# Split SiLU-multiply: the first tile's store as one DMA over 128 partitions instead of five strided pieces

## The chip, the cores and the metric

The kernel runs on one core of a Trainium2 chip. The metric is device time in microseconds (us) of one execution. Three runs of the kernel before gave 470.19, 470.32 and 470.40 us; the median is 470.32 us.

The core has engines that work side by side, each with its own instruction stream: ScalarE (ACT in the profile) for activation functions, VectorE (DVE) for elementwise work, SyncE (SP), which here only starts transfers, and two that do nothing that matters here. Sixteen DMA engines move data between the device memory (HBM) and the on-chip memory of 128 partitions (SBUF). A transfer is started by an instruction on SP or ACT; SP's transfers stand in the queue that the profile calls q1, ACT's in q10, and both queues are worked off by the same sixteen engines.

## The reference

The input `x` has the shape 32 x 512 x 2048 in float32. With `x1` the first 1024 columns and `x2` the last 1024:

```python
silu_x1 = x1 * (1 / (1 + np.exp(-x1)))
return (silu_x1 * x2).astype(np.float32)
```

So 134.2 MB are read, each element once, and 67.1 MB are written.

## The kernel before

The 32 x 512 rows are taken as 16384 rows of 2048 numbers and cut into 16 tiles of 1024 rows. A tile lies on 128 partitions with K = 8 rows on each, so partition p of a tile holds eight neighbouring rows of the input: 64 KB in one piece on the way in, and 32 KB on the way out, since the output rows are half as long. A load is thus 8 MB, a store 4 MB. There are two input buffers `xt` and two output buffers `ot` (lines 58 and 59).

The order of the work is written out by hand in the loop (lines 101 to 120), and each engine executes its own instructions in that order:

- `load(i)` (line 82) is issued by SP. `load(0)` and `load(1)` come ahead of the loop; `load(0)` is even moved ahead of the program's first barrier (line 10). In tile i, after the store, `load(i + 2)` is issued; it goes into the buffer that tile i has just been read from, so it waits for tile i's last multiplication.
- `silu` (line 86) runs on ACT, from `xt` into `ot`. It waits for the load of its tile and, from tile 2 on, for the store of tile i - 2, which has to have left the `ot` buffer.
- `mul` (line 93) runs on DVE, in place on `ot`, with the second half of `xt`.
- the store (line 112) is issued by ACT, after the tile's last multiplication. ACT works in order, so the next tile's `silu` comes behind this issue.

Tile 0 is computed in four chunks of two rows (`KC_EDGE = 2`), tiles 1 to 14 in one piece, and tile 15 in two halves (`KS = 4`) with a store for each half (line 120).

The store of tile 0 alone is split. The list `OPENING` (line 49) has five pairs of a partition slice and a row slice. In order, the pieces are: rows 0 and 1 of every fourth partition from 0 (32 partitions, 256 KB); rows 0 to 3 of every fourth partition from 2 (512 KB); rows 4 to 7 of the same partitions (512 KB); rows 2 to 7 of every fourth partition from 0 (768 KB); and all rows of the odd partitions (64 partitions, 2048 KB). The first piece needs only the first chunk of tile 0 and the second only the first two chunks, so these can be issued before the tile is complete. With the five pieces the program has 37 DMAs: 16 loads, 5 pieces, 14 whole stores and 2 half stores.

Of the kernel before, what the change touches and what calls it, by code (L numbers as in the profile page):

```python
# [1 line left out]

# [4 lines left out]


def issue_ahead_of_the_first_barrier(nc):

    head, body = nc.main_func.blocks[:2]
    load = next(ins for ins in body.instructions if type(ins).__name__ == "InstDMACopy")
    at = next(
        j for j, ins in enumerate(head.instructions)
        if ins.engine == load.engine and type(ins).__name__ == "InstDrain"
    )
    body.instructions = [ins for ins in body.instructions if ins.name != load.name]  # L20
    head.instructions = head.instructions[:at] + [load] + head.instructions[at:]


@with_exitstack
def kernel(
    ctx: ExitStack,
    tc: tile.TileContext,
    x: bass.AP,
    out: bass.AP,
):  # L30

    nc = tc.nc
    P = nc.NUM_PARTITIONS

    x_flat = x.flatten_outer_dims()  # L40
    out_flat = out.flatten_outer_dims()
    num_rows, in_cols = x_flat.shape
    half = in_cols // 2
    dt = x_flat.dtype

    K = 8
    KC_EDGE = 2
    KS = 4
    OPENING = [
        (slice(0, None, 4), slice(0, 2)),  # L50
        (slice(2, None, 4), slice(0, 4)),
        (slice(2, None, 4), slice(4, None)),
        (slice(0, None, 4), slice(2, None)),
        (slice(1, None, 2), slice(None)),
    ]
    PLAN = [K] * (num_rows // (P * K))

    in_pool = ctx.enter_context(tc.tile_pool(name="in_pool", bufs=2))
    out_pool = ctx.enter_context(tc.tile_pool(name="out_pool", bufs=2))

    plan = []
    row = 0
    for k in PLAN:
        plan.append((row, k))
        row += P * k
    assert row == num_rows
    n_tiles = len(plan)

    def view(flat, i):
        row0, k = plan[i]  # L70
        return flat[row0:row0 + P * k].rearrange("(p k) d -> p k d", k=k)

    nc.at_finalize(issue_ahead_of_the_first_barrier)


    ctx.enter_context(tc.manual_schedule())

    loaded = {}

    def load(i):  # L80
        xt = in_pool.tile([P, K, in_cols], dt, name="xt")
        nc.sync.dma_start(out=xt[:, :plan[i][1], :], in_=view(x_flat, i))
        loaded[i] = xt

    def silu(ot, xt, c, ce):
        nc.scalar.activation(  # L86
            out=ot[:, c:ce, :],
            in_=xt[:, c:ce, :half],
            func=mybir.ActivationFunctionType.Silu,
        )  # L90

    def mul(ot, xt, c, ce):
        nc.vector.tensor_mul(  # L93
            out=ot[:, c:ce, :],
            in0=ot[:, c:ce, :],
            in1=xt[:, c:ce, half:],
        )

    load(0)
    load(1)  # L100
    for i in range(n_tiles):
        xt = loaded.pop(i)
        ov = view(out_flat, i)
        ot = out_pool.tile([P, K, half], dt, name="ot")
        if i < n_tiles - 1:
            kc = KC_EDGE if i == 0 else K
            for c in range(0, K, kc):
                silu(ot, xt, c, c + kc)
                mul(ot, xt, c, c + kc)

            for ps, ks in OPENING if i == 0 else [(slice(None), slice(None))]:
                nc.scalar.dma_start(out=ov[ps, ks], in_=ot[ps, ks])
            if i + 2 < n_tiles:
                load(i + 2)
            continue
        for c in range(0, K, KS):
            silu(ot, xt, c, c + KS)
            mul(ot, xt, c, c + KS)
        for c in range(0, K, KS):
            nc.scalar.dma_start(out=ov[:, c:c + KS], in_=ot[:, c:c + KS])  # L120


# [1 line left out]
_INS = ['x']  # L124
_OUTS = [((32, 512, 1024), 'float32')]


# [23 lines left out]
```

## Time and profile before

| what | value |
|---|---|
| median of three runs (lowest, highest) | 470.32 us (470.19, 470.40) |
| span of the profiled execution, first to last instruction | 468.39 us |
| that span below the median of the runs | 1.93 us |
| time of all packets, as a share of 16 DMA engines over the span | q1 66.4%, q10 33.2% |
| mean rate | 430 GB/s |
| DVE busy, ACT busy | 139.3 us, 114.1 us |
| idle time of ACT that a store's landing ended | 305.8 us, 14 times |
| from issue to landing, median | load 35.1 us, whole store 42.2 us |
| `silu` of a whole tile, `mul` of a whole tile | 7.03 us, 8.69 us |

For the profiled execution the span is given and no device time of its own; what lies around the span is taken as the 1.93 us between it and the median of the runs. All times inside an execution count from the span's start.

A few terms. A packet is what one DMA engine moves at a stretch: in a load, one partition's 64 KB; in a whole store, one partition's 32 KB. With 128 partitions over 16 engines each engine has 8 packets of every load and of every whole store. Behind them each engine has one more record of 4 bytes, which reports that the engine's part is done; it is called the closing entry here. So a load or a whole store is 9 entries on each engine, and its landing is the report of the last of the 16. In the view of the DMA queues, "packets" counts the entries of all sixteen engines that start in the chosen window.

### The profile page before, as it was taken

How to read it: one execution, taken by the hardware profiler on the slowest of the kernel's cores; microseconds unless marked ns; L12 is line 12 of the kernel's file. 1: busy time of each engine (PE TensorE's matmuls, PEld its weight loads, DVE VectorE, ACT ScalarE, POOL GpSimd, SP SyncE). 2: the span in 40 equal slices, each digit the busy share in tenths (PEclk: the TensorE clock that was granted, in tenths of full speed). 3: DMA queues.
4: the chain of work that ended last, by engine and by line, in shares of the span. 5: the costliest groups of instructions: out<-in, count | busy, mean ns of one | idle time of the engine just before them, and what ended most of it. 6: DMA issues, size and time to landing. Idle time of an engine off the chain costs nothing.

```text
span 468.4 us, 185 instructions
## 1 busy us (share of the span) xinstructions
DVE 139.3 (30%) x20; ACT 114.1 (24%) x21; POOL 0.2 (0%) x4
## 2 busy tenths in 40 slices
DVE  0070600704207042070520605116061150602543
ACT  1142305005050050601406014060230602306060
POOL 0000000000000000000000000000000000000000
DMA  9899999999999999999999999899999899999998
GB/s 442 364 470 425 448 403 403 493 403 403 448 465 431 403 442 409 493 403 414 437 448 448 403 448 465 386 448 439 411 493 442 372 439 493 403 448 403 428 423 358
DMA packets 4880, 201.33 MB, mean 430 GB/s; under 512 B 592, under 2 KB 592, under 8 KB 592
## 3 DMA queue, kind: packets, MB, share of 16 engines
q1 hardware_dynamic: 2304, 134.22, 66.4%
q10 hardware_dynamic: 2576, 67.11, 33.2%
HBM read 134.22 MB, written 67.11 MB: 430 GB/s over the span
## 4 chain that ended last, share of the span: by engine, by line
DMA 72%; DVE 14%; ACT 11%; DVEq 1%; issue 0%
DMA out_dram<-ot 63%; DVE ot L93 14%; ACT ot L86 11%; DMA xt<-in_x_dram 9%; DVEq L146 1%
## 5 line engine op out<-in xcount | busy, mean ns | idle before, releaser
L93 DVE TENSOR_TENSOR ot<-ot,xt 128x8192 f32<-128x8192 f32 (+2 forms) x20 | 139.3, 6983 | 321.1 <-ACT ot L86 321.1
L86 ACT ACTIVATE ot<-xt 128x8192 f32<-128x8192 f32 (+2 forms) x20 | 112.8, 5661 | 340.2 <-DMA out_dram<-ot 305.8
L86 ACT ACT_TABLE_LOAD x1 | 1.3, 1283 | 0.8 <-PEq L135 0.8
L135 POOL MEMSET const-bfloat16-1.0<- 128x1 bf16 x1 | 0.1, 102 | 0.0
L135 POOL MEMSET const-uint8-127<- 128x1 uint8 x1 | 0.1, 102 | 0.0
L135 POOL MEMSET const-float32-1.0<- 128x1 f32 x1 | 0.1, 99 | 0.0
L135 POOL MEMSET const-float32-0.0<- 128x1 f32 x1 | 0.1, 98 | 0.2 <-issue 0.2
## 6 DMA issues: line engine op xcount, KB each, us to landing
out_dram<-ot ACTq DMA_DIRECT2D x14, 4096.0 KB, 42.2
out_dram<-ot ACTq DMA_DIRECT2D x3, 2048.0 KB, 6.9
out_dram<-ot ACTq DMA_DIRECT2D x2, 512.0 KB, 17.6
out_dram<-ot ACTq DMA_DIRECT2D x1, 768.0 KB, 28.2
xt<-in_x_dram SPq DMA_DIRECT2D x16, 35.1
out_dram<-ot ACTq DMA_DIRECT2D x1, 256.0 KB, 11.3
```

Of the source, the lines that this page charges most:

```text
L86: nc.scalar.activation(out=ot[:, c:ce, :], in_=xt[:, c:ce, :half], func=mybir.ActivationFunctionType.Silu,)
L93: nc.vector.tensor_mul(out=ot[:, c:ce, :], in0=ot[:, c:ce, :], in1=xt[:, c:ce, half:],)
L135: nc = _bacc.Bacc("TRN2", target_bir_lowering=False, num_devices=1)
L146: with _tile.TileContext(nc) as tc:
```

## The change

The list `OPENING` goes, and tile 0 is stored like tiles 1 to 14: one DMA over all 128 partitions, issued after the tile's last multiplication. The four chunks in which tile 0 is computed stay. The program has 33 DMAs.

```diff
-    OPENING = [
-        (slice(0, None, 4), slice(0, 2)),
-        (slice(2, None, 4), slice(0, 4)),
-        (slice(2, None, 4), slice(4, None)),
-        (slice(0, None, 4), slice(2, None)),
-        (slice(1, None, 2), slice(None)),
-    ]
     PLAN = [K] * (num_rows // (P * K))
...
-            for ps, ks in OPENING if i == 0 else [(slice(None), slice(None))]:
-                nc.scalar.dma_start(out=ov[ps, ks], in_=ot[ps, ks])
+            nc.scalar.dma_start(out=ov, in_=ot)
             if i + 2 < n_tiles:
                 load(i + 2)
             continue
```

## The prediction

> **What bounds the kernel now.** I read the page first: the DMA row and the queue rows.
>
> ```profile
> span 468.4 us, 185 instructions
> ...
> DMA  9899999999999999999999999899999899999998
> ...
> q1 hardware_dynamic: 2304, 134.22, 66.4%
> q10 hardware_dynamic: 2576, 67.11, 33.2%
> ```
>
> The 16 DMA engines are busy 99.6% of the span. The bytes do not change, so the kernel can become slower only where these engines run dry, and faster only by what they lose besides moving bytes. The place where they could run dry is the end, so I read the timeline there: after the last load nothing but stores is left, and the two half stores of tile 15 must be computed while older stores keep the engines busy.
>
> ```profile
> 439.57 0.34 ACTq L112 DMA_DIRECT2D out_dram<-ot  x1
> 448.01 7.12 ACT L86 ACTIVATE ot<-xt 128x4096 f32<-128x4096 f32 x2 [17.20 <-DMA out_dram<-ot]
> 451.66 8.76 DVE L93 TENSOR_TENSOR ot<-ot,xt 128x4096 f32<-128x4096 f32 x2 [12.13 <-ACT ot L86]
> 456.12 4.67 ACTq L120 DMA_DIRECT2D out_dram<-ot  x2
> ```
>
> The last tile's silu starts at 448.01, its first half store is issued 8.11 us later, and the packet records have its first packet 0.85 us after that, at 456.97. Tile 14's store ends at 456.85 on the first of the engines and at 457.29 on the last. The gap is at most 0.12 us: the cover just suffices. So the question is how many store packets are left when the last load is in.
>
> Next I read the queues with windows, to see how they share an engine. From 20.9 to 31 us:
>
> ```profile
> q1 hardware_dynamic: 80, 4.19, 99.0%
> ...
> out_dram<-ot ACTq DMA_DIRECT2D x1, 512.0 KB, 15.7
> out_dram<-ot ACTq DMA_DIRECT2D x1, 256.0 KB, 11.3
> ```
>
> 80 load entries, 5 on each engine (load 0's closing entry and four packets of load 1), and no row for q10, though two pieces were issued in this window. From 31 to 443.5 us:
>
> ```profile
> q1 hardware_dynamic: 2080, 121.64, 68.1%
> q10 hardware_dynamic: 2080, 57.15, 32.1%
> ```
>
> 2080 entries each, 130 on each engine: the queues take strict turns, one entry each, closing entries included. From 444.7 to 445.3 us:
>
> ```profile
> q10 hardware_dynamic: 16, 0.52, 202.3%
> q1 hardware_dynamic: 16, 0.00, 1.5%
> ```
>
> Here the last load closes, with 0.00 MB: its 16 closing entries (the packet records: at 444.75 on the first engine, 445.19 on the last; landing 445.54).
>
> **A count that fixes the end.** Each engine has 16 x 9 = 144 load entries. n of them have gone by when the first store packet gets its turn; from there each load entry goes with one store entry. So when load 15 closes, 144 - n store entries are done. Before, n = 8 (load 0) + 5 = 13, so 131. Up to and including tile 14 there are 17 entries of the five pieces (12 packets of 8 to 32 KB, 5 closing entries: 272 of the page's 2576 over 16) and 14 x 9 = 126, in all 143. Left: 12 entries, of which 10 are packets of 32 KB and two close. The records show just these: from the closing of load 15 to tile 14's end is 457.29 - 445.19 = 12.10 us, 10 packets of 1.21.
>
> After the change, tiles 0 to 14 have 15 x 9 = 135 store entries. Left when load 15 closes: 135 - (144 - n) = n - 9, one of them closing: **r = n - 10 packets**, instead of 10. The four missing closing entries and the four missing small packets bring the store queue eight turns forward; a later start gives some back.
>
> **What n becomes.** The first piece was issued at 26.02 and moved first at 31.02 to 31.42 (16 engines). The new store is issued at 32.62, when the last multiplication of tile 0 ends; that is when the third piece is issued now, and nothing ahead of it changes (DVE runs its four chunks back to back). Until it joins, loads go on alone at 2.418 us a packet: packet ends at 30.72, 33.14, 35.56, 37.98, 40.39 (0.39 later on the last engine) mean n = 13, 14, 15, 16, 17. How long a whole store needs to join a running load queue is not in the trace. The nearest row is the first piece: it missed the turn 2.29 to 2.67 us after its issue and took the one at 5.00 to 5.40. The lower bound from elsewhere is the 0.85 us of the first half store, on engines that had nothing else to do. For the new store the turn at 35.56 to 35.95 is 2.94 to 3.33 us after issue, that at 37.98 to 38.37 is 5.36 to 5.75. By the first piece the delay lies between 2.67 and 5.00, so the second turn is safe and the first is reached only by a delay under 3.33, which is (3.33 - 2.67) / 2.33 = 28% of that stretch. I take the second: **n = 16, r = 6**. Ends kept: n = 15 and n = 17.
>
> **The sum.**
> 1. Load 15 closes later by the (10 - 6) store packets that now come before it: 4 x 1.213 = 4.85 us. It lands at 445.54 + 4.85 = 450.39.
> 2. Today the last silu waits for tile 13's store (447.99) and not for the load. With r = 6 that store is out earlier, so the load decides: the silu starts at 450.41 instead of 448.01, and the first half store's first packet comes at 456.97 + 2.40 = 459.37.
> 3. All bytes up to tile 14 are still moved by 456.85 to 457.29, so the engines idle for about 2.1 us (last engine) to 2.4 us (first). The half stores then run as now. The last engine sets the end, but also starts level with the others: before, starts 0.33 us apart became ends 0.21 apart (466.81 to 467.02). From 459.37, 9.72 to 9.84 us of packets give 469.09 to 469.21 against 467.02: **+2.1 to +2.2, taken as +2.15 us**, at most 2.40.
> 4. Off it goes what the pieces cost the DMA engines. Three rounds of load packets around the pieces take 2.704, 2.606 and 2.709 us instead of 2.418 (those that start at 28.30, 31.32 and 36.64), 0.77 us in all; whole stores later show nothing of the kind. The new store is also the first to join, so one excess of 0.29 may stay: I take -0.48, bounds 0 and -0.77.
> 5. ACT saves four issues: the five take 0.55 + 0.48 + 0.48 + 0.62 + 0.63 us, one whole store 0.36. It then waits 14.73 us for load 1, which hides this: 0. Closing entries take 0.009 us each: 0. Load 2's issue on SP waits for the same multiplication, at 32.62: 0. Compute in the middle: a tile's store is issued 15.79 us after its silu starts, and r + 1 = 7 entries of the older store, in turns of 3.63 us with loads, cover 25.4 us: 0; with r = 5 still 21.8.
>
> Sum: 468.39 + 2.15 - 0.48 = 470.06 for the span, and with the 1.93 us around it **472.0 us** (470.32 + 1.67 = 471.99). Bounds of this case: 470.32 + 2.15 - 0.77 = 471.7 and 470.32 + 2.40 = 472.7.
>
> The Trainium skill, "DMA: Bandwidth & Descriptors", section "Rules for kernel authors", advises one 128-partition transfer where transfers to disjoint partitions share the engines, so by it the change is right or neutral; that weighs each DMA, not the order in which two queues drain. The same page, "Queues, rings and completion order", has an engine drain a packet of some 9 to 17 descriptors from one queue before it switches; the rows above differ, one entry each. If a whole DMA of 9 entries went per turn, tile 14's whole store would be left at the end, the loss would vanish, and the time would be about 470.
>
> **The rivals.**
> - *The store joins a turn earlier on at least one engine* (n = 15, r = 5). The landing of each load waits for its slowest engine, so one engine is enough. One more packet, 1.21 us: 471.99 + 1.21 = 473.2 (bounds 472.9 to 473.9). For it: the turns of the 16 engines are spread over 0.39 us, and 2.94 is near 2.67. Against: most of the possible delays.
> - *Earlier still* (n = 14): +1.21 again, 474.4. It needs a delay under 0.9 us, which only the idle engines of the tail show.
> - *A turn later* (n = 17, r = 7): 1.21 less, 470.8. The delay must exceed 5.36 us; the first piece allows at most 5.40 on its last engine, and a store of 128 rows may be slower to start.
> - *The other side: the tail stays covered.* The place is the wait before the last silu. With r = 8 or more the load no longer decides: (10 - 8) x 1.213 = 2.43 us, just the 2.45 between load 15's and store 13's landings. Then only step 4 remains: 470.32 - 0.48 = 469.8 (469.6 to 470.3). It decides from n = 18 on: the store would have to miss the turn at 40.4 too, some 7.8 us after its issue, or the middle would have to reset the order of the queues. Against: no wait there leaves an engine idle now, so nothing resets it. That the pieces do nothing for the end gives the same numbers.
>
> **How the numbers follow.** Chances: r = 6, 0.50; r = 5, 0.30; r = 4, 0.05; r = 7, 0.07; tail covered or no effect, 0.08. A measurement of this kernel tells about 0.2% (0.94 us) from no change. The first three are slower by more than that: 0.85. r = 7 (+0.5) lies within it, as does most of the last case: 0.13 same. Faster by over 0.94 us would need more than all of the 0.77: 0.02. The likeliest gives 472.0. The range: r = 6 and r = 5 hold 0.80 and reach from 471.7 to 473.9; since the low side has more cases I go down to 471.0, into r = 7, and up to 474.0.
>
> **What would show it.** In the changed kernel: q10's first packets at 37.98 to 38.4 (35.6 would be the first rival, 40.4 the third); load 15's landing near 450 (449.9 with step 4) and the last silu released by the load, no longer by a store; the chain through the loads; some 2 us without any packet near 457 to 459; one long load packet before the first store packet instead of three. Wrong would be: the last silu still released by a store, the queues not in strict turns, or a dry stretch in the middle.

## The result and the profile after

The changed kernel takes 473.38 us (median of 14 runs, 473.01 to 474.15); beside it the kernel before took 470.33 us (14 runs). The ratio is 1.0057, with a 95% interval of 1.0041 to 1.0073: 3.05 us slower by the medians, where 1.67 were forecast. The direction and the range held (471.0 to 474.0); the likeliest case was 1.4 us too low. In the experiments below, two of the twelve runs of two by rows (486.0 and 486.5 us) were disturbed and are left out of its ratio and range, and beside the last three kernels some runs of the kernel before were long (up to 477.19 us), which pulls their ratios below what the medians give. The profiled execution of the changed kernel took 473.47 us with a span of 471.14 us.

The page after, its DMA row and its queues:

```profile
span 471.1 us, 177 instructions
...
DMA  9999999999999999999999899999999999999978
...
q1 hardware_dynamic: 2304, 134.22, 66.1%
q10 hardware_dynamic: 2448, 67.11, 33.0%
```

The store queue has 128 entries fewer (8 on each engine, as counted), the bytes are the same, and the slice that lost is the last but one, 7 where there was a 9. The timeline after, from tile 14's last multiplication:

```profile
437.90 0.34 ACTq L104 DMA_DIRECT2D out_dram<-ot  x1
451.04 7.12 ACT L79 ACTIVATE ot<-xt 128x4096 f32<-128x4096 f32 x2 [21.89 <-DMA xt<-in_x_dram]
454.69 8.76 DVE L86 TENSOR_TENSOR ot<-ot,xt 128x4096 f32<-128x4096 f32 x2 [16.82 <-ACT ot L79]
459.15 4.67 ACTq L112 DMA_DIRECT2D out_dram<-ot  x2
```

Tile 14's store is even issued 1.67 us earlier than before (437.90 against 439.57), but the last silu starts 3.03 us later, and what releases it is now the load and no longer a store. In the list of waits this has turned round for the whole kernel; the line that named the stores with 305.8 us is gone, and this one stands in its place (total, times, longest):

```profile
ACT ot L79 <- DMA xt<-in_x_dram: 343.3, 16, 22.2
```

The window of the DMA queues from 457.9 to 459.9 us shows the dry stretch at the end; no engine starts anything:

```profile
DMA packets 0, 0.00 MB, mean 0 GB/s; under 512 B 0, under 2 KB 0, under 8 KB 0
```

By the packet records the engines run dry at 456.86 (the first) to 457.87 (the last), and the first half store moves at 459.99 to 460.14. And the window of the opening, 32.9 to 38.7 us, from the store's issue at 32.91 to just ahead of its first packet at 38.76:

```profile
q1 hardware_dynamic: 32, 2.10, 98.4%
```

Two load packets on each engine and no store: the store missed the turn 2.6 to 3.3 us after its issue and took the next. From there both queues have the same number of entries again (38.7 to 448.3 us):

```profile
q1 hardware_dynamic: 2032, 118.49, 66.7%
q10 hardware_dynamic: 2032, 59.25, 33.5%
```

Equal counts over so long a window do not yet show turns of single entries; two queues that took turns with whole DMAs of 9 entries would give them too. A window of one turn (2.418 + 1.213 us) decides that. From 200 to 203.63 us, in the kernel before as in the changed one:

```profile
q1 hardware_dynamic: 16, 1.05, 66.6%
q10 hardware_dynamic: 16, 0.52, 33.4%
```

That is one packet of each queue for each of the sixteen engines.

### The profile page after: what moved, and what is told of

Read it like the earlier page. It is cut to its first block, busy times and chain, and to the rows that moved or that the text cites. A ratio compares the mean times of both kernels' runs of the same rounds, so it can differ in the third digit from the quotient of the medians.

```text
span 471.1 us, 177 instructions
## 1 busy us (share of the span) xinstructions
DVE 139.4 (30%) x20; ACT 114.1 (24%) x21; POOL 0.2 (0%) x4
## 3 DMA queue, kind: packets, MB, share of 16 engines
q10 hardware_dynamic: 2448, 67.11, 33.0%
## 4 chain that ended last, share of the span: by engine, by line
DMA 72%; DVE 14%; ACT 11%; DVEq 1%; issue 0%; ACTq 0%
DMA xt<-in_x_dram 72%; DVE ot L86 14%; ACT ot L79 11%; DVEq L138 1%; ACTq L79 0%
```

## The experiments

The theory under test: the two queues take turns entry by entry, closing entries included, and the time follows from r, the store packets left on an engine when its last load closes. The rival that the numbers so far did not exclude: the early issue of the first two pieces is what the five pieces were worth. All times are medians; r is counted in the packet records of the profiled run, on each engine from its closing of load 15 to the end of its part of tile 14's store; one number means that all sixteen engines have it. The records do not name the engine; its packets are followed from the end of one to the start of the next. Beside the first four kernels the kernel before took 470.27 us, beside the next four 470.41, beside the last three 470.40.

| kernel | first store | us (lowest to highest) | r | first half store issued |
|---|---|---|---|---|
| before | five pieces, two of them early | 470.33 | 10 | 456.12 |
| changed | one DMA | 473.38 (473.01 to 474.15) | 6 | 459.15 |
| two by partition | halves of neighbouring partitions | 475.83 (475.76 to 476.33) | 7 | 461.66 |
| three by partition | 64, 32, 32 neighbouring partitions | 473.24 (472.67 to 473.65) | 8 | 459.13 |
| two by rows | rows 0 to 3, rows 4 to 7 | 471.05 (470.77 to 473.71) | 8 | 459.47 |
| quarters at the end | one DMA | 470.64 (470.33 to 471.08) | 6 | 455.09 |
| two by every second | even, odd partitions | 472.65 (471.76 to 472.92) | 7 | 457.61 |
| three by stride | even, two of every fourth | 470.59 (470.29 to 470.75) | 8 | 456.71 |
| load 7 in two | one DMA | 476.98 (476.38 to 478.10) | 6; 5 on two engines | 462.50 |
| five pieces late | five pieces, none early | 473.24 (472.88 to 475.12) | 8 | 459.20 |
| tile 0 in halves | one DMA, issued 1.35 us later | 472.78 (471.76 to 474.08) | 7 | 458.01 |
| tile 0 whole | one DMA, issued 4.86 us later | 471.05 (470.92 to 471.43) | 8 | 456.93 |
| tile 7 in three | one DMA; tile 7's store in three | 470.43 (470.24 to 471.60) | 8 | 456.95 |

The issue times are those of one profiled run each; its time can lie at either end of the range (473.71 for two by rows, 471.86 for two by every second).

### Is the loss at the end? Quarters at the end

```diff
-    KS = 4
+    KS = 2
```

> The changed kernel, one DMA for the first store, but the last tile computed and stored in quarters of two rows (KS = 2). The first quarter's store can be issued about 1.9 + 2.3 = 4.2 us after the last silu starts instead of 8.1. Turn theory: still 6 packets left (7.3 us), while now about 0.4 + 4.2 + 0.9 = 5.5 us have to be covered, so the dry stretch goes and the time falls to 470.3 to 470.9. Rival (the loss lies in the opening, in the long packet before the first store packet, or in the middle): at most a few tenths change, 473.0 to 473.6.

Measured: 470.64 us, ratio to before 1.0008 (1.0000 to 1.0017). Nothing of the opening or the middle was touched. In its timeline:

```profile
450.82 5.51 ACT L79 ACTIVATE ot<-xt 128x2048 f32<-128x2048 f32 x3 [21.95 <-DMA xt<-in_x_dram]
452.76 8.89 DVE L86 TENSOR_TENSOR ot<-ot,xt 128x2048 f32<-128x2048 f32 x4 [15.17 <-ACT ot L79]
455.09 0.34 ACTq L112 DMA_DIRECT2D out_dram<-ot  x1
```

The last silu starts as late as in the changed kernel (450.82), but a store is issued 4.3 us after it instead of 8.1, and its first packet follows tile 14's last directly, at 456.94. So 2.7 of the 3.05 us lie in the dry stretch at the end; what a later last load cost is repaired by a shorter last step.

### Is it the count of entries? Two by every second, three by stride

```diff
-            nc.scalar.dma_start(out=ov, in_=ot)
+            for ps in [slice(0, None, 2), slice(1, None, 2)] if i == 0 else [slice(0, P)]:
+                nc.scalar.dma_start(out=ov[ps], in_=ot[ps])
```

Both are issued after the last multiplication of tile 0. The page of this kernel counts 2464 store entries against 2448, one closing entry more on each engine.

> [...] Turn theory: 7 packets left when the last load closes on an engine, 1.21 us less than the changed kernel: 472.2 (471.8 to 472.6), the engines about 1 us apart as there. Rival (bytes issued early are what counts): 473.4. Second rival (any split of the first store throws the engines apart, as in the halves of neighbouring partitions): 475 or more.

Three by stride is the same with `[slice(0, None, 2), slice(1, None, 4), slice(3, None, 4)]`; its page counts 2480 store entries, two closing entries more on each engine than in the changed kernel.

> [...] Turn theory: 8 packets left, 2.4 us less than the changed kernel: 471.0 (470.6 to 471.4). Rival (early bytes): 473.4. Second rival (any split throws the engines apart): 473 or more.

Measured: 472.65 (ratio 1.0041, 1.0029 to 1.0054) and 470.59 (0.9994, 0.9979 to 1.0008). Two steps of a turn each: r is 7 and 8, and the last stores are issued 1.5 and 2.4 us earlier than in the changed kernel. Two by every second:

```profile
449.51 7.12 ACT L79 ACTIVATE ot<-xt 128x4096 f32<-128x4096 f32 x2 [21.96 <-DMA xt<-in_x_dram]
453.16 8.76 DVE L86 TENSOR_TENSOR ot<-ot,xt 128x4096 f32<-128x4096 f32 x2 [16.88 <-ACT ot L79]
457.61 4.67 ACTq L113 DMA_DIRECT2D out_dram<-ot  x2
```

Three by stride:

```profile
448.60 7.12 ACT L79 ACTIVATE ot<-xt 128x4096 f32<-128x4096 f32 x2 [21.98 <-DMA xt<-in_x_dram]
452.25 8.76 DVE L86 TENSOR_TENSOR ot<-ot,xt 128x4096 f32<-128x4096 f32 x2 [16.91 <-ACT ot L79]
456.71 4.67 ACTq L113 DMA_DIRECT2D out_dram<-ot  x2
```

The packets of the first store are the same 32 KB ones in all three kernels, and nothing is issued early. What two more DMAs add is two closing entries of 0.009 us on each engine, and with them the kernel is as fast as before. The rival falls. The runs of two by every second lie in two groups, 471.8 and 472.6 to 472.9; why was not followed up.

### Does the place matter? Tile 7 in three

The same three slices, with `if i == 7`.

> The changed kernel with one whole store for each tile except tile 7, whose store goes out as three DMAs (even partitions, then two sets of every fourth). Turn theory: two closing entries more anywhere ahead of tile 14 do what they do in the first store: 8 packets left, 470.5 to 471.2, as with the first store in three. Rival (only the opening decides): 473.4. A possible miss: if the 16 engines do not all shift by the same turn, some lose up to 1.2 us to others, as with load 7 in two.

Measured: 470.43 us; ratio 0.9983 (0.9957 to 1.0010). The opening is that of the changed kernel, its last silu:

```profile
448.84 7.12 ACT L79 ACTIVATE ot<-xt 128x4096 f32<-128x4096 f32 x2 [21.90 <-DMA xt<-in_x_dram]
```

It starts 2.2 us earlier than in the changed kernel. So the opening is not special: two entries in tile 7's store count as two in tile 0's do. No kernel of this study is clearly faster than the kernel before.

### Does a later start help? Tile 0 in halves, tile 0 whole

```diff
-    KC_EDGE = 2
+    KC_EDGE = 8
```

For tile 0 in halves it is 4.

> The changed kernel, one DMA for the first store, but tile 0 computed in two chunks of four rows instead of four of two, so its store is issued some 1.6 us later (about 34.4 us). Turn theory: the turn at 38.0 to 38.4 us comes 3.6 to 4.0 us after issue, the one at 40.4 comes 6.0 us after. The changed kernel's store missed a turn 2.6 to 3.3 us after issue, the first piece of the kernel before took one at 5.0. So either still 6 packets are left (473.4) or 7 (472.2). Rival (a late first store is what costs): 1.6 us more, about 475.

> The changed kernel, one DMA for the first store, but tile 0 computed in one piece, so its store is issued at about 37.6 us, 4.7 us later than in the changed kernel. Turn theory: the store queue starts two to three turns later, after load 1 has closed, so 8 or 9 packets are left when the last load closes, the tail is covered and the kernel becomes faster than the changed one by doing its first tile later: 470.3 to 471.0. Rival (a late first store is what costs): slower than 473.4, up to 478.

Measured: 472.78 (ratio 1.0027, 0.9995 to 1.0059) and 471.05 (0.9991, 0.9959 to 1.0023). Tile 0 whole:

```profile
37.77 19.66 SPq L75 DMA_DIRECT2D xt<-in_x_dram  x2
37.77 0.38 ACTq L104 DMA_DIRECT2D out_dram<-ot  x1
...
448.82 7.12 ACT L79 ACTIVATE ot<-xt 128x4096 f32<-128x4096 f32 x2 [22.00 <-DMA out_dram<-ot]
```

The first store is issued at 37.77 instead of 32.91, the last silu starts 2.2 us earlier, released by a store again, and the kernel gains 2.3 us on the changed one by doing its first tile later. Tile 0 in halves missed the turn 3.6 to 4.1 us after issue and has r = 7 in the profiled run (472.00 us); its twelve runs spread from 471.76 to 474.08, so not all of them need have the same r.

### The other sign: load 7 in two

```diff
-        nc.sync.dma_start(out=xt[:, :plan[i][1], :], in_=view(x_flat, i))
+        for ps in [slice(0, None, 2), slice(1, None, 2)] if i == 7 else [slice(0, P)]:
+            nc.sync.dma_start(out=xt[ps, :plan[i][1], :], in_=view(x_flat, i)[ps])
```

> The changed kernel with one whole store for each tile, but load 7 as two DMAs, even and odd partitions: one closing entry more in the load queue. Turn theory, with the opposite sign: one more store entry is let by before the last load closes, so 5 packets are left and the dry stretch grows by 1.21 us: 474.6 (474.2 to 475.0). Rivals (the opening alone decides; or fewer and larger DMAs are what costs): no change, 473.4.

Measured: 476.98 us, ratio 1.0141 (1.0124 to 1.0157). The time moved the way that was expected, but by 3.6 us and not by 1.2, and not for the reason that was expected. From 206.7 to 211.8 us, after load 7's first half has closed:

```profile
DMA packets 34, 1.18 MB, mean 231 GB/s; under 512 B 16, under 2 KB 16, under 8 KB 16
...
q1 hardware_dynamic: 18, 1.18, 72.0%
q10 hardware_dynamic: 16, 0.00, 0.2%
```

The store queue has run dry: 16 closing entries and no store packet, though tile 6's store was issued at 205.78; it moves at 211.87, 6.1 us after its issue. So the count does not run through from the opening. At the end r is still 6 on fourteen engines and 5 on two, where 5 was expected on all. From 204 to 214 us packets are 1.4 us longer than usual, on the mean of the engines. After that the engines no longer go in step: the landing of a load takes 2.85 us from its first engine to its last (248.46 to 251.31), against about 1.0 in the changed kernel, and each silu waits for the last. At load 15 this adds up to the time found: on the mean of the engines it closes 1.9 us later than in the changed kernel, and its last engine is 2.2 us behind that mean instead of 0.8, together 3.3 of the 3.6 us. Why the engines fell apart stays open.

### Too far the other way: five pieces late

```diff
     OPENING = [
-        (slice(0, None, 4), slice(0, 2)),
-        (slice(2, None, 4), slice(0, 4)),
-        (slice(2, None, 4), slice(4, None)),
-        (slice(0, None, 4), slice(2, None)),
+        (slice(0, None, 4), slice(6, 8)),
+        (slice(2, None, 4), slice(4, 8)),
+        (slice(2, None, 4), slice(0, 4)),
+        (slice(0, None, 4), slice(0, 6)),
         (slice(1, None, 2), slice(None)),
     ]
```

> The kernel before with the same five pieces in size, order and partitions, but the row slices of the first, second and fourth mirrored so that each piece holds rows of the last chunk: all five are issued only after the last multiplication of tile 0. Turn theory: 17 store entries for tile 0 as before, started three turns later, so more than 10 packets are left, the last silu waits for tile 13's store, and the time is that of the kernel before: 470.3 (470.0 to 470.8). Rival (early bytes): about 473.4.

Measured: 473.24 us, ratio 1.0069 (1.0050 to 1.0087): the theory's number missed, and the rival's was hit. The timeline shows that it is not for the rival's reason:

```profile
83.35 7.03 ACT L86 ACTIVATE ot<-xt 128x8192 f32<-128x8192 f32 x1 [34.24 <-DMA out_dram<-ot]
90.41 8.69 DVE L93 TENSOR_TENSOR ot<-ot,xt 128x8192 f32<-128x8192 f32 x1 [32.58 <-ACT ot L86]
99.13 0.33 SPq L82 DMA_DIRECT2D xt<-in_x_dram  x1
99.14 0.36 ACTq L112 DMA_DIRECT2D out_dram<-ot  x1
```

With 17 entries and a late start the store queue is so far behind that tile 2 waits for tile 0's store until 83.35. Load 4 waits for tile 2's last multiplication, until 99.13, but load 3 has landed by 94.13. The load queue is dry, and from 93.5 to 100 us only stores move:

```profile
q10 hardware_dynamic: 82, 2.16, 77.1%
q1 hardware_dynamic: 2, 0.00, 0.0%
```

The stores are served alone until they too run out; the engines idle for about 1 us (store packets end at 99.14 to 99.83, the next load packets start at 100.10 to 100.83), and these take 3.93 us instead of 2.42. That is 2.5 of the 2.8 us, and it is lost in the middle; at the end r is 8. I had put no bound on the other side: 12 entries left when the last load closes are still good (the kernel before), while the start of this kernel, with 16 load entries gone by ahead of 17 store entries, would leave 143 - 128 = 15 and starves the loads.

### Splits that throw the engines apart

```diff
-            nc.scalar.dma_start(out=ov, in_=ot)
+            for ps in [slice(0, 64), slice(64, 128)] if i == 0 else [slice(0, P)]:
+                nc.scalar.dma_start(out=ov[ps], in_=ot[ps])
```

Three by partition has `[slice(0, 64), slice(64, 96), slice(96, 128)]`.

> The changed kernel with the first store as two DMAs, partitions 0 to 63 and 64 to 127, both issued after the last multiplication of tile 0; same packets, one closing entry more on each engine. Turn theory: each store entry ahead of tile 14 moves the store queue back by one turn, so 7 packets of 32 KB are left when the last load closes instead of 6, and the dry stretch shrinks by 1.21 us: 472.2. Rival (what counted was that some bytes of the first store were issued 4 to 6 us early): nothing is issued early, so 473.4 stays.

> The first store as three DMAs of 64, 32 and 32 neighbouring partitions, all after the last multiplication: two closing entries more than the changed kernel. Turn theory: 8 packets left, two times 1.21 us less: 471.0, with a dry stretch of 0.6 us or less. Rival (early bytes): 473.4.

Measured: 475.83 (ratio 1.0119, 1.0105 to 1.0134) and 473.24 (1.0062, 1.0050 to 1.0074), 3.2 and 2.7 us above the strided splits with the same number of entries. The count holds here too. In two by partition load 15 closes at 449.78 on the first engine and 453.11 on the last, and on each engine tile 14's store ends 8.48 us after that, 7 packets of 1.21; in three by partition it is 9.7 us, 8 packets. What differs is when load 15 closes. The first load packets left aside, the packets of a whole run add up to 3.6 and 2.6 us more than usual, on the mean of the engines, against 1.0 and 1.1 in the strided splits; store packets of 1.3 to 1.7 us instead of 1.213, between 43 and 68 us, are among them. And the last load's landing takes 3.3 and 1.9 us from the first engine to the last, against 0.5 in both strided ones. Together these make the last closing of load 15 4.1 and 2.5 us later than in the strided splits; the profiled runs differ by 4.0 and 2.5 us. So r alone does not give the time: three by partition and three by stride both have r = 8 and lie 2.7 us apart. That the halves give an engine other partitions than a whole store does, and the strided sets do not, would explain it; the records do not show which engine moves which partition, so this is argued, not shown.

Two by rows:

```diff
-            nc.scalar.dma_start(out=ov, in_=ot)
+            for c in (0, 4) if i == 0 else (0,):
+                ce = c + 4 if i == 0 else K
+                nc.scalar.dma_start(out=ov[:, c:ce], in_=ot[:, c:ce])
```

> The first store as two DMAs over all 128 partitions, rows 0 to 3 and rows 4 to 7, both after the last multiplication: 18 store entries on each engine instead of 9 (16 packets of 16 KB, two closing). Turn theory: nine turns back, 16 entries left when the last load closes, so the last silu waits for tile 13's store again, the tail is covered and the time is that of the kernel before: 470.3 (470.0 to 470.8). Rival (early bytes): 473.4.

Measured: 471.05 us, ratio 1.0018 (1.0006 to 1.0030). The kernel was not quite what the expectation says: its first half was issued at 28.63, when rows 0 to 3 were done, not after the last multiplication, so it does not speak against the early bytes. Nor are 16 entries left at the end: r is 8 on every engine, and the reason is that of five pieces late. Tile 2's silu waits for tile 0's store until 81.57, so load 4 is issued at 97.35, while load 3 has landed at 96.01. Until then only stores move (95.8 to 99.3 us):

```profile
q10 hardware_dynamic: 44, 1.44, 95.3%
```

Here the stores last until load 4 comes, so the engines do not idle; but the order of the queues starts anew. The profiled run (473.71 us) lies 2.7 us above the median. In it one engine closes load 15 at 450.81 and the other fifteen by 448.24; no run at the median was profiled.

## Why the prediction was right or wrong

**The count held.** n = 16, r = 6, the last silu released by the load, one long packet ahead of the first store instead of three: all as forecast. On the mean of the sixteen engines load 15 closed 4.90 us later (449.60 against 444.75 on the first); step 1 of the sum has 4.85. Seven more kernels have the r that n and the entries give: 7 and 8 for one and two entries more (8 wherever the two stand, and with neighbouring partitions as with strided ones), 7 and 8 where the first store joins one and three load entries later (tile 0 in halves with n = 17, tile 0 whole with n = 19, where the tenth entry left is tile 13's closing one). The count fails where a queue runs dry on the way: load 7 in two, two by rows, five pieces late. The delay that a store needs before it can take a turn, bounded by 2.67 and 5.00 us, was over 2.6 us on the first engine and 3.3 on the last in the changed kernel, and over 3.6 and 4.1 in tile 0 in halves.

**The time was partly luck.** 473.38 us is the number of the first rival (r = 5, 473.2 us), and it lies 0.7 us above 472.7, the most that the sum's own bounds allow. It is inside the range only because that range left room for r = 5. The records decide against this rival: r is 6 on all sixteen engines. So the mechanism was right, and the sum was too small in the terms that follow.

**Step 4 was wrong.** It took 0.48 us off for the pieces' long packets. The one store costs the same in a single packet: the load packet ahead of it took 3.27 us instead of 2.418, 0.85 more, against 0.77 for three rounds before. So the saving was -0.09 instead of 0.48, a miss of 0.57 and outside the bounds of the step; it is also why the first store packets came at 38.76 to 39.52 us and not at 37.98 to 38.4. In the other kernels whose tile 0 is stored after its last multiplication the long packet costs 0.9 to 1.2 us; five pieces late spend 0.7 on several packets.

**The size of step 1 was wrong on the last engine.** I carried over a spread of 0.44 us between the engines. In the changed kernel they are 0.68 apart after the first packet and 1.01 at the end, so load 15's last engine closed at 450.61, 5.42 us later and not 4.85. As the last silu waits for the last engine, this counts in full: with step 4's 0.09 already told, 0.48 more. Not all of this is the change's doing: 0.68 us of the spread stand when load 0 closes (20.99 to 21.68), before any instruction that the change touches, and at the end one engine stands 0.5 us behind the others (450.60; the other fifteen closed load 15 by 450.08). How much of it returns from run to run is not shown.

**Step 3** let the engines' spread shrink to gain 0.25 us in the half stores; they gained 0.05. With the wait of the silu (0.06) and the end of the span (0.22 nearer to the last packet) the span's miss is 1.08 us: 2.75 measured, 1.67 forecast. Another 0.40 lies outside the span: 2.33 us around the profiled run, and about 2.3 to 2.5 in all 14, against the 1.93 that I carried over. It goes with the number of DMAs: the kernels with 35 or 37 have about 1.7 to 2.0 us, those with 33 or 34 about 2.0 to 2.5. What links the two is open, but it was no constant.

**The rivals.** The one that a turn earlier or later decides was the right shape: tile 0 in halves and tile 0 whole are its later cases. The covered tail came out as put: from r = 8 on the time is that of the kernel before or up to 0.8 us more, but for five pieces late and three by partition, which lose time ahead of the tail. What I had not seen is that the cover has an upper end too (five pieces late, two by rows).

**The two rules of the Trainium skill** that the prediction weighed: "DMA: Bandwidth & Descriptors", section "Rules for kernel authors", says of two transfers to disjoint partition halves that one 128-partition transfer should be used instead. For the lower and the upper half this case agrees, 475.83 us against 473.38; even and odd partitions (472.65) and three strided sets (470.59) do not. By the counts above that is a matter of the queues' order and not of the speed of a transfer. The section "Queues, rings and completion order" of the same page has an engine drain a packet of typically 9 to 17 descriptors from one ring before it switches; here one turn is a single entry of each queue, as the window from 200 to 203.63 us shows.

## What to carry to other kernels

Where two DMA queues are both full, as here, they advance in step, entry by entry, and the order they start in is the order they end in, as long as neither runs dry: look at the end of the kernel and count what is left in each queue when the last load closes, against the time from that landing to the first store that depends on it. If the cover is short by a few packets, a shorter last step, one or two more DMAs in the queue that should lag (strided sets here; with neighbouring partitions the gain was lost again ahead of the tail), or a later start of that queue are all the same remedy; too much lag starves the other queue through the buffers. A landing is that of the slowest engine: in the changed kernel one of sixteen held the last silu back by 0.5 us.

## What the runs showed of the hardware

- A closing entry of 4 bytes takes 0.009 us and takes a turn of its own: two more of them on each engine moved the end by 2.8 us (473.38 to 470.59).
- A queue that was empty got its first turn late while the other queue was busy: 5.0 us after issue in the kernel before and in five pieces late, 5.9 in the changed one, 6.1 in load 7 in two and 7.3 in tile 0 in halves, against 0.85 us on idle engines. The load packet ahead of it was 0.9 to 1.2 us longer than its usual 2.418 where the first store packets were of 32 KB, and 0.05 to 0.3 us longer where they were smaller (kernel before, two by rows, five pieces late); the load queue's own restart in five pieces late cost 1.5.
- Which partitions go together in a DMA matters for the engines' step: even and odd partitions 472.65 us, lower and upper half 475.83 us, with the same entries.
